# Expert stage of a one-core network: routing ahead of the token split, gathers of four experts, sixteen weight buffers, and a written order for TensorE

## The chip, the cores and the metric

The kernel runs as one program on one core of a Trainium2 chip. The metric is the device time of one execution in microseconds. The kernel before takes 2054.01 us, the median of 3 runs (2053.54 to 2054.9).

## The reference, cut to what matters

256 tokens of width 1024 go through a first block (two layers, each a gated feed-forward part, a mixer of a state space scan and dilated attention, and a second feed-forward part) and then a second block. The second block computes a hybrid mixer of a convolution and a gated linear attention, and ends like this:

```python
h = h + ga1[:, None, :] * y                 # y: the mixer's w_out product
u2 = modulate(rmsnorm(h, g_norm2[l]), sh2, sc2)
y2 = hierarchical_moe(u2, ...)              # 4 groups of 8 experts
h = h + ga2[:, None, :] * y2
...
return modulate(rmsnorm(h, g_final), shf, scf)

# in hierarchical_moe, t = u2 as 256 tokens:
gsel = top_k(t @ w_rg + b_rg, 1)            # a group for each token
top_v, top_i = lax.top_k(le_sel, TOP_K)     # two of the group's 8 experts
w = jax.nn.softmax(top_v, axis=-1) * wg
for e in range(N_EXPERTS):
    hid = jax.nn.silu(t @ w1[e]) * (t @ w3[e])
    y = y + comb[:, e:e + 1] * (hid @ w2[e])
```

There are 32 experts with a hidden width of 512, so w1, w3 and w2 of one expert are 2 MB each in fp32.

## The kernel before, in words

The dense part (first block, and the second up to `w_out`) streams fp32 weights through a ring of 1 MB buffers called `raw`, splits each in a high and a low part (`hi` on ScalarE, `lo` on VectorE) and sums three products in PSUM. The change leaves it nearly as it is. Its last product is `w_out` of the second block (in `mixer2`, from L957): two pieces of 512 columns, each of 256 token rows. Behind each piece come the residual (L968, L969), the product with the router's gain row (L971), the turn to columns on TensorE (L974) and the router's logits (L980). Then `rsqrt` gives the norm's factor on VectorE (three Newton steps, L84 to L86), and L989 scales the logits.

**Routing** (`route`, L1197) is one chain on VectorE over the 36 logits of each token: the best group, the best and second expert, their sum as a one-hot mask (L1234); two matmuls (L1237, L1238) count each token's place in its expert, and L1240 gives `pos`. **norm2** (L1329) writes the normed tokens `u` (L1335, the shift row `sh2` added), their high part `u2h` on ScalarE and the low part `u2l` on GpSimd (L1341). `moe_final` calls norm2 between the creation of the routing chain and its first step, and the instructions stand in that order on VectorE.

**The gather** (L1412): from `pos`, L1417 writes one-hot matrices `sel` for a batch of 8 experts with 64 slots each (512 columns). For each of 8 pieces of 128 features, four matmuls (`u2h` and `u2l`, two token halves, 512 columns) pick the tokens, and the result is copied to `T`. Four batches serve 32 experts.

**The experts** (L1530) are taken two at a time, 16 pairs. For each pair `project` runs w1 and w3 (L1469), `hidden` turns the results (L1484) and writes H with Silu and a product, and `down` runs w2 of the pair before (L1504). Its products have 64 slots as the stationary tile, the two experts side by side in the array. `spread` adds the results, as high and low part `yh` and `yl`, to the tokens with `selT` (L1522). A pair has 12 loads of 1 MB: two halves of two buffers (one for each expert) for each of w1, w3, w2. `halves` asks for two new loads when it has used two buffers:

```python
for i in range(2):
    yield i, (self.loaded.pop(0), self.loaded.pop(0))
    self.refill(2)
    self.tick()
```

The order on the engines is chosen by a scheduler at build time. Side work (gathers, `slots`, spreads) is handed to it as generators that `tick` advances beside the products.

**Weight buffers.** The 1 MB buffers of the expert stage are in four pools: RAW2 = 3 and RAW3 = 2 that open during the mixer, RAWB = 4 taken over from the dense ring, RAW4 = 3 that open when the dense part's memory is free: 12. A load is issued on SP's queue (L1392) when its buffer is free, in program order.

**The end.** `finish` (L1358) multiplies the sum by `ga2`, adds it to `x`, squares, `rsqrt`, and writes the output with the rows `Gf` and `shf`. `finish_rows` (L1343) loads these rows on GpSimd's queue right behind the routing and forms `Gf` there.

## Time and profile before

| | |
|---|---|
| median of 3 runs | 2054.01 us |
| profiled execution | 2053.34 us, its span 2051.6 us |
| PE busy | 1967.1 us (96%) |
| VectorE (DVE) busy | 1226.8 us (60%) |
| ScalarE (ACT) busy | 882.6 us (43%) |
| GpSimd (POOL) busy | 138.5 us (7%) |
| expert weights | 192 loads of 1024 KB |
| DMA in the last eight of 40 slices | 414 to 421 GB/s in six of them, 378 and 369 in the others but the last |

The expert stage begins at about 1524 us of the span. Ahead of it TensorE is the busy engine and the DMA moves 97 to 283 GB/s in a slice of 51 us; in it both are close to full. The page's share for PE is an average over both.

### The profile page before, as it was taken

How to read it: one execution, taken by the hardware profiler on the slowest of the kernel's cores; microseconds unless marked ns; L12 is line 12 of the kernel's file. 1: busy time of each engine (PE TensorE's matmuls, PEld its weight loads, DVE VectorE, ACT ScalarE, POOL GpSimd, SP SyncE). 2: the span in 40 equal slices, each digit the busy share in tenths (PEclk: the TensorE clock that was granted, in tenths of full speed). 3: DMA queues.
4: the chain of work that ended last, by engine and by line, in shares of the span. 5: the costliest groups of instructions: out<-in, count | busy, mean ns of one | idle time of the engine just before them, and what ended most of it. 6: DMA issues, size and time to landing. Idle time of an engine off the chain costs nothing. (4 is left out here: it accounts for less than half of the span.)

```text
span 2051.6 us, 25322 instructions
## 1 busy us (share of the span) xinstructions
PE 1967.1 (96%) x9734; PEld 1436.8 (70%) x9734; DVE 1226.8 (60%) x2099; ACT 882.6 (43%) x1318; POOL 138.5 (7%) x226
## 2 busy tenths in 40 slices
PE   8999999999999999999999999999969999999996
PEld 6888978788888888887788888978754333333332
DVE  5884897778867775698866555999772111110113
ACT  5444676654444444575745444576522101111101
POOL 1000222000000000014000000000120000000001
PEclk9999999999999999999999999999989999999998
DMA  8885543447776885642446556544766999999994
GB/s 281 280 283 185 166 144 103 154 155 266 263 258 207 266 271 182 196 150 97 133 144 204 179 164 204 177 148 140 244 261 269 422 414 378 421 369 420 421 421 172
DMA packets 193100, 493.11 MB, mean 240 GB/s; under 512 B 11832, under 2 KB 47600, under 8 KB 168400
## 3 DMA queue, kind: packets, MB, share of 16 engines
q1 hardware_dynamic: 185760, 479.32, 64.6%
q0 software_dynamic: 4992, 11.49, 1.7%
q8 instruction: 78, 1.28, 0.2%
q10 hardware_dynamic: 2224, 0.66, 0.2%
q14 instruction: 46, 0.38, 0.1%
HBM read 490.34 MB, written 1.08 MB: 240 GB/s over the span
## 5 line engine op out<-in xcount | busy, mean ns | idle before, releaser
L128 DVE TENSOR_TENSOR lo<-raw,hi 128x1024 fp32r<-128x1024 f32 (+1 forms) x462 | 563.6, 1221 | 280.4 <-ACT hi L127 279.4
L127 ACT ACTIVATE hi<-raw 128x1024 fp32r<-128x1024 f32 (+1 forms) x462 | 486.6, 1055 | 548.4 <-PE mm L174 477.9
L172 PE MATMUL mm<-hi,xh 128*128 128x512 f32 (+2 forms) x1200 | 463.9, 388 | 3.7 <-ACT hi L127 3.7
L173 PE MATMUL mm<-lo,xh 128*128 128x512 f32 (+2 forms) x1200 | 458.3, 382 | 0.4 <-DVE lo L128 0.4
L174 PE MATMUL mm<-hi,xl 128*128 128x512 f32 (+2 forms) x1200 | 457.8, 381 | 0.0
L172 PEld LDWEIGHTS mm<-hi,xh 128*128 128x128 f32 x1200 | 226.0, 189 | 49.2 <-ACT hi L127 4.6
L173 PEld LDWEIGHTS mm<-lo,xh 128*128 128x128 f32 x1200 | 226.2, 188 | 46.3 <-DVE lo L128 2.0
L174 PEld LDWEIGHTS mm<-hi,xl 128*128 128x128 f32 x1200 | 226.0, 188 | 46.0
L1469 PE MATMUL mm<-raw,T 128*64 128x512 f32 x1024 | 242.4, 596 | 0.0
L1469 PEld LDWEIGHTS mm<-raw,T 128*64 128x64 f32 x1024 | 72.9, 137 | 139.8 <-issue 137.0
L1504 PE MATMUL mm<-raw,H 128*64 128x512 f32 x512 | 148.6, 600 | 10.1 <-DVE gu L1474 10.1
L172 PE MATMUL mm<-hi,hh 128*128 128x512 f32 x352 | 139.1, 395 | 0.0
L174 PE MATMUL mm<-hi,hl 128*128 128x512 f32 x352 | 138.8, 394 | 0.0
L173 PE MATMUL mm<-lo,hh 128*128 128x512 f32 x352 | 138.5, 394 | 0.0
L1474 DVE COPY gu<-mm 128x512 f32<-128x512 f32 x16 | 11.1, 692 | 178.6 <-PE mm L1469 168.8
L1504 PEld LDWEIGHTS mm<-raw,H 128*64 128x64 f32 x512 | 45.9, 136 | 85.6 <-issue 63.3
L1512 ACT ACTIVATE yh<-mm,wsl 128x512 fp32r<-128x512 f32 x32 | 22.0, 687 | 181.7 <-PE mm L1504 181.7
L190 PE MATMUL mm<-xl,hi 128*128 128x256 f32 x320 | 90.0, 282 | 0.4 <-DVE xl L204 0.4
L189 PE MATMUL mm<-xh,hi 128*128 128x256 f32 x320 | 89.7, 282 | 0.0
L191 PE MATMUL mm<-xh,lo 128*128 128x256 f32 x320 | 89.7, 281 | 0.0
L759 DVE SCALAR_TENSOR_TENSOR macc<-raw,cact,macc 128x512 f32<-128x512 f32 x112 | 83.9, 750 | 2.2
L1513 DVE SCALAR_TENSOR_TENSOR yl<-mm,wsl,yh 128x512 fp32r<-128x512 f32 x32 | 24.0, 751 | 94.3 <-ACT yh L1512 93.0
(428 smaller groups left out, 2642.6 us busy)
## 6 DMA issues: line engine op xcount, KB each, us to landing
raw<-in_w_dram SPq DMA_DIRECT2D x192, 1024.0 KB, 10.2
raw<-in_w_in_dram SPq DMA_DIRECT2D x71, 1024.0 KB, 5.2
raw<-in_ffn_w_up_dram SPq DMA_DIRECT2D x44, 1024.0 KB, 7.0
raw<-in_ffn_w_gate_dram SPq DMA_DIRECT2D x43, 1024.0 KB, 5.2
raw<-in_ffn_w_down_dram SPq DMA_DIRECT2D x40, 1024.0 KB, 5.1
raw<-in_w_ada_dram SPq DMA_DIRECT2D x24, 1024.0 KB, 5.3
raw<-in_w_out_dram SPq DMA_DIRECT2D x20, 1024.0 KB, 5.1
raw<-in_w_ada_f_dram SPq DMA_DIRECT2D x8, 1024.0 KB, 5.3
```

The source lines that it names most:

```text
L127: nc.scalar.activation(h, r, AF.Copy)
L128: nc.vector.tensor_tensor(l, r, h.bitcast(F32), op=ALU.subtract)
L172: nc.tensor.matmul(ps[t][:, :w], xh[:, kc, sl], hi, start=kc == 0, stop=False)
L173: nc.tensor.matmul(ps[t][:, :w], xh[:, kc, sl], lo, start=False, stop=False)
L174: nc.tensor.matmul(ps[t][:, :w], xl[:, kc, sl], hi, start=False, stop=kc == kt - 1)
L189: nc.tensor.matmul(o, hi[:, sl], xh[:, kc, :], start=kc == 0, stop=False)
L190: nc.tensor.matmul(o, hi[:, sl], xl[:, kc, :], start=False, stop=False)
L191: nc.tensor.matmul(o, lo[:, sl], xh[:, kc, :], start=False, stop=kc == kt - 1)
L759: last = nc.vector.scalar_tensor_tensor(acc, raw[:, k, :], c, acc, op0=ALU.mult, op1=ALU.add)
L1469: nc.tensor.matmul(pg[s * CAP : (s + 1) * CAP, :], x[:, kc, s, :], w[:, k, :], start=kc == 0, stop=kc == KD - 1,)
L1504: nc.tensor.matmul(pd[nb][q, :], H[:, c, q], w[s][:, k, nb * 512 : (nb + 1) * 512], start=c == 0, stop=c == 3,)
L1513: nc.vector.scalar_tensor_tensor(yl, pd[nb], ws, yh.bitcast(F32), op0=ALU.mult, op1=ALU.subtract)
```

## The change

- Constants: a batch is 4 experts (256 columns for a gather), 16 weight buffers (RAW2 = 4, RAW4 = 6).
- `w_out` of the second block runs as 512, 256 and 256 columns, so the residual, turn and logits of the last piece have half the size. `rsqrt` has seven operations for its steps where it had nine.
- The routing chain stands right behind the logits. `u2h` is written from `xg` on ScalarE with the norm's factor as scale, in four pieces of 512, and `u2l` on VectorE (`low`) in four pieces of 512, one of them while TensorE counts places and three behind `sel`. The shift `sh2` is now a column of 128x8 and is added when a gather's PSUM result is copied to `T`. Nothing of this is on GpSimd.
- The first gather uses four PSUM banks at a time, `u2h` ahead of `u2l`.
- TensorE's order in the expert stage is the program's own (`manual_schedule`), and the side work stands at fixed hooks between halves. Spreads run behind the first half of the next pair's w1.
- `finish_rows` stands behind the last pair's projections, loads its rows on SP's queue into two buffers of the weight ring, and forms `Gf` with one VectorE operation per row. `finish` uses the memory of `u2h` and `u2l`.

```diff
-RAW2 = 3
+RAW2 = 4
 RAW3 = 2
-RAW4 = 3
-BATCH = 8
+RAW4 = 6
+BATCH = 4
...
-        for _ in range(3):
-            nc.vector.tensor_mul(t, y, y)
-            nc.vector.scalar_tensor_tensor(t, t, -0.5, m, op0=ALU.mult, op1=ALU.mult)
-            nc.vector.scalar_tensor_tensor(y, t, 1.5, y, op0=ALU.add, op1=ALU.mult)
+        nc.vector.tensor_mul(t, y, y)
+        nc.vector.scalar_tensor_tensor(t, t, -0.703952253 * RC, m, op0=ALU.mult, op1=ALU.mult)
+        nc.vector.scalar_tensor_tensor(y, t, 0.703952253 * 2.38924456 * RC, y, op0=ALU.add, op1=ALU.mult)
+        nc.vector.tensor_mul(t, y, y)
+        nc.vector.tensor_mul(t, t, m)
+        nc.vector.scalar_tensor_tensor(t, t, -10.0 / 3 * RC**2, t, op0=ALU.add, op1=ALU.mult)
+        nc.vector.scalar_tensor_tensor(y, t, 5.0 * RC**4, y, op0=ALU.add, op1=ALU.mult)
...
+            for i, (c0, w) in enumerate(((0, 512), (512, 256), (768, 256))):
+                sl = slice(c0, c0 + w)
+                n = w // P
+                ps = self.gemm_x(a["w_out_2"][0], c0, w, self.xh, self.xl)
...
-        nc.vector.tensor_add(mb, o1, o2)
+        done = nc.vector.tensor_add(mb, o1, o2).ins
 
         pp = self.t(self.mm, [P, 512], "mm")
         nc.tensor.matmul(pp[:, 0:64], self.tri_le, mb, start=True, stop=False)
         nc.tensor.matmul(pp[:, 32:64], self.ones, mb[:, 0, :], start=False, stop=True)
+        with self.tc.issue_after(done):
+            lows.pop(0)()
...
+        self.xg = self.t(self.s2, [P, 2, D], "T")
+        self.sh2 = self.t(self.const, [P, KD], "cact")
...
-            self.norm2(lp, u2h, u2l)
+            lows = self.norm2(u2h, u2l)
+            route = self.route(lp, lows)
             pos = next(route)
-            rows = self.finish_rows(lp)
-            comb, cnt = self.experts(lp, u2h, u2l, route, pos, acc)
+            with tc.manual_schedule(engines={mybir.EngineType.PE}):
+                comb, cnt, rows = self.experts(lp, u2h, u2l, lows, route, pos, acc)
...
-            nc.vector.scalar_tensor_tensor(
-                u.rearrange("p (k q) -> p q k", k=KD), self.xg[:, t, :].rearrange("p (q k) -> p q k", k=KD),
-                self.rstd[:, t : t + 1], self.sh2.rearrange("p (q k) -> p q k", k=KD),
-                op0=ALU.mult, op1=ALU.add,
...
+            return lambda: nc.vector.scalar_tensor_tensor(
+                l, u, r, h.bitcast(F32), op0=ALU.mult, op1=ALU.subtract
             )
-            nc.scalar.activation(u2h[:, t, :], u, AF.Copy)
-            nc.gpsimd.tensor_tensor(u2l[:, t, :], u, u2h[:, t, :].bitcast(F32), op=ALU.subtract)
-
-    def finish_rows(self, lp):
+
+        lows = []
+        for k0 in range(0, KD, 4):
+            for t in range(2):
+                h, l = (
+                    x[:, t, k0 * P : (k0 + 4) * P].rearrange("p (k q) -> p k q", k=4) for x in (u2h, u2l)
+                )
+                u = self.xg[:, t, :].rearrange("p (q k) -> p k q", k=KD)[:, k0 : k0 + 4, :]
+                r = self.rstd[:, t : t + 1]
+                nc.scalar.activation(h, u, AF.Copy, scale=r)
+                lows.append(low(h, u, l, r))
+        return lows
...
+            w = self.eraw().rearrange("p a b -> p (a b)").rearrange("p (k n) -> p k n", n=D)
+            rows += [w[:, 0, :], w[:, 1, :]]
...
+            nc.sync.dma_start(dst, self.modd[0:1, idx * D : (idx + 1) * D].to_broadcast([P, D]))
+        g = rows.pop()
+        nc.sync.dma_start(g, a["g_final_2"].rearrange("(o n) -> o n", o=1).to_broadcast([P, D]))
+        nc.vector.scalar_tensor_tensor(rows[1], rows[1], 1.0, g, op0=ALU.add, op1=ALU.mult)
...
-            self.tick()
-
-    def gather(self, pool, b, u2h, u2l, pos, out, banks=None):
+            for f in hooks[i] if hooks else ():
+                f()
...
+        with self.tc.issue_after(i.ins):
+            for low in lows:
+                low()
...
+        for k0 in range(0, KD, n_k):
+            pgs = banks or [self.t(self.tp, [P, 512], "tp")]
+            pgs = [x[:, : BATCH * CAP].rearrange("p (e s) -> p e s", e=BATCH) for x in pgs]
             for n, src in enumerate((u2h, u2l)):
-                for t in range(2):
-                    nc.tensor.matmul(
-                        pg, src[:, t, sl], sel[:, t], start=n == 0 and t == 0, stop=n == 1 and t == 1
-                    )
-            if kc % 2:
-                nc.vector.tensor_copy(T[:, kc], pg)
-            else:
-                nc.scalar.activation(T[:, kc], pg, AF.Copy)
+                for kc, pg in enumerate(pgs, k0):
+                    sl = slice(kc * P, (kc + 1) * P)
+                    for t in range(2):
+                        nc.tensor.matmul(
+                            pg, src[:, t, sl], sel[:, t], start=n == 0 and t == 0, stop=n == 1 and t == 1
+                        )
+            for kc, pg in enumerate(pgs, k0):
+                sh = self.sh2[:, kc : kc + 1]
+                if kc % 2:
+                    nc.vector.tensor_scalar(T[:, kc], pg, sh, None, op0=ALU.add)
+                else:
+                    self.filled = nc.scalar.activation(T[:, kc], pg, AF.Identity, bias=sh).ins
...
+            gu.append(self.project(pool, x, on_scalar, [spread], [some(gat, 2 if ei else 3)]))
+            if e == 0:
+                with self.tc.issue_after(filled):
+                    comb, combs, cnt = next(route)
+            slots = self.slots(pool, sel, ei, e, combs, so)
+            gu.append(
+                self.project(pool, x, nc.vector.tensor_copy, [some(turns, 1), some(slots, 1)], [])
+            )
             if last:
-                self.down(pool, e - 2, last[0][0], *last[1], acc)
-            for _ in hid:
-                pass
+                spread = self.down(
+                    pool, e - 2, last[0][0], *last[1], acc, [some(turns, 1), some(gat, 1)], [some(gat, 1)]
+                )
+            else:
+                next(turns)
             last = h, so
-        self.drain()
-        self.down(pool, NEXP - 2, last[0][0], *last[1], acc)
-        self.drain()
-        return comb, cnt
+        rows = self.finish_rows()
+        spread_end = self.down(pool, NEXP - 2, last[0][0], *last[1], acc, [spread], [])
+        spread_end()
```
TensorE, in a pair's w1/w3 and the w2 products of the pair before; `raw` is a weight buffer, `H` the hidden values, `mm` a PSUM result of one half of w2's columns, `tp` a turn or a gather. Before:

```order
L1504 MATMUL mm_14549<-raw_14434,H_14422 64x512
L1504 MATMUL mm_14550<-raw_14434,H_14422 64x512
L1484 MATMUL tp_14583<-csq_66,gu_14540 128x128 x4
L1446 MATMUL tp_14606<-identr_320,sel_13752 128x128 x2
L1448 MATMUL tp_14606<-combs_13699,sel_13752 128x4 x2
L1504 MATMUL mm_14549<-raw_14436,H_14422 64x512
L1504 MATMUL mm_14549<-raw_14434,H_14422 64x512
L1504 MATMUL mm_14549<-raw_14436,H_14422 64x512
L1504 MATMUL mm_14550<-raw_14436,H_14422 64x512
```
After:

```order
L1528 MATMUL mm_14061<-raw_13867,H_13876 64x512
L1528 MATMUL mm_14061<-raw_13869,H_13876 64x512
L1528 MATMUL mm_14061<-raw_13867,H_13876 64x512
L1528 MATMUL mm_14061<-raw_13869,H_13876 64x512
L1528 MATMUL mm_14062<-raw_13867,H_13876 64x512
L1528 MATMUL mm_14062<-raw_13869,H_13876 64x512
L1528 MATMUL mm_14062<-raw_13867,H_13876 64x512
L1528 MATMUL mm_14062<-raw_13869,H_13876 64x512
L1509 MATMUL tp_14075<-csq_66,gu_14059 128x128 x4
L1455 MATMUL tp_14081<-sel_13999,u2h_13613 128x256 x2
L1455 MATMUL tp_14081<-sel_13999,u2l_13614 128x256 x2
```
Before, the first two rows use the buffer of the same expert, and `raw_14434` and `raw_14436` (the two experts of the pair) alternate irregularly around the turns. After, the two buffers alternate in every row of a half, and turns and gathers stand between halves.

SP's queue where the last `w_out` weights and the first expert weights (`in_w_2`) are issued. Before:

```order
L156 DMA raw_13344<-in_w_out_dram 128x4x512
L156 DMA raw_13419<-in_w_out_dram 128x4x512
L1392 DMA raw_13152<-in_w_2_dram 128x2048
L1392 DMA raw_13154<-in_w_2_dram 128x2048
L1392 DMA raw_13156<-in_w_2_dram 128x2048
L156 DMA raw_13453<-in_w_out_dram 128x4x512
```
After:

```order
L162 DMA raw_13309<-in_w_out_dram 128x4x512
L1410 DMA raw_13115<-in_w_2_dram 128x2048
L1410 DMA raw_13117<-in_w_2_dram 128x2048
L1410 DMA raw_13119<-in_w_2_dram 128x2048
L1410 DMA raw_13121<-in_w_2_dram 128x2048
L162 DMA raw_13384<-in_w_out_dram 128x8x256
L162 DMA raw_13468<-in_w_out_dram 128x8x256
```
Four expert loads stand ahead of the last `w_out` loads where three stood, and these are two of 256 columns where one of 512 stood behind them.

VectorE from the logits `lg` to the one-hot `sel`. Before:

```order
L989 SCALAR_TENSOR_TENSOR lg_13536<-ax_13305,nw_y_13524,wr_13158 128x36
L989 SCALAR_TENSOR_TENSOR lg_13536<-ax_13306,nw_y_13524,wr_13158 128x36
L1335 SCALAR_TENSOR_TENSOR T_13580<-T_13150,nw_y_13524 128x128x8 x2
L1211 TENSOR_REDUCE rgm_13588<-lg_13536 128x2
L1212 TENSOR_TENSOR gu_13587<-lg_13536,rgm_13588 128x8
```
After:

```order
L998 SCALAR_TENSOR_TENSOR lg_13565<-ax_13271,nw_y_13555,wr_13123 128x36
L1220 TENSOR_REDUCE rgm_13620<-lg_13565 128x2
...
L1243 TENSOR_TENSOR gu_13619<-gu_13619 128x64
L1346 SCALAR_TENSOR_TENSOR u2l_13614<-T_13112,nw_y_13555,u2h_13613 128x512
L1251 TENSOR_TENSOR pos_13648<-mm_13644,gu_13619 128x64
L1436 TENSOR_TENSOR sel_13652<-cmisc_316,pos_13648 128x256 x2
L1346 SCALAR_TENSOR_TENSOR u2l_13614<-T_13112,nw_y_13555,u2h_13613 128x512 x3
```
The two L1335 operations ahead of the chain are gone; one `u2l` piece stands in front of `pos`, in the time of the count on TensorE, and three stand behind the first `sel`.

## Rows read from the trace of the kernel before

**Rows 1.** The page: its first line, and the DMA issues (x, KB, us to landing).
```profile
span 2051.6 us, 25322 instructions
...
raw<-in_w_dram SPq DMA_DIRECT2D x192, 1024.0 KB, 10.2
```
**Rows 2.** Busy time by stretch: length, PE, PEld, DVE, ACT, POOL, PEclk, DMA share, GB/s.
```profile
1528.00:1556.00 28.00, 15.60 (x62) 10.45 (x64) 18.06 (x41) 5.91 (x11) 11.05 (x8) 0.68 0.07 19
1556.00:1560.00 4.00, 4.00 (x22) 1.40 (x20) 0.32 (x2) 0.60 (x1) 0.00 (x0) 1.00 0.99 340
1800.00:1900.00 100.00, 94.85 (x395) 36.06 (x392) 12.36 (x22) 10.05 (x17) 0.00 (x0) 1.00 0.97 394
1900.00:2010.00 110.00, 104.94 (x453) 39.78 (x454) 12.10 (x23) 11.81 (x20) 0.00 (x0) 1.00 1.01 421
2018.60:2020.00 1.40, 1.40 (x9) 0.56 (x6) 0.00 (x0) 0.00 (x0) 0.00 (x0) 1.00 0.26 105
```
**Rows 3.** PE's timeline at the start of the expert stage: start us, us, what.
```profile
1539.75 0.69 PE L1237 MATMUL mm<-gu,csq 128*128 128x64 f32 x2 [15.69 <-DVE gu L1234]
...
1551.36 3.65 PE L1469 MATMUL mm<-raw,T 128*64 128x512 f32 x16
```
**Rows 4.** DVE's timeline from the last residual to the one-hot matrices.
```profile
1516.30 0.69 DVE L968 TENSOR_TENSOR xg<-mm,gain 128x512 f32<-128x512 f32 x1 [7.45 <-PE mm L174]
...
1523.09 0.16 DVE L86 SCALAR_TENSOR_TENSOR nw_y<-nw_t,nw_y 128x2 f32<-128x2 f32 x1
...
1524.27 3.77 DVE L1335 SCALAR_TENSOR_TENSOR T<-T,nw_y 128x1024 f32<-128x1024 f32 x2
...
1528.10 2.05 DVE L1212 TENSOR_TENSOR gu<-lg,rgm 128x8 f32<-128x8 f32 x1
...
1533.99 0.22 DVE L1212 TENSOR_TENSOR gu<-gu,r1m 128x64 f32<-128x64 f32 x1
...
1539.47 0.22 DVE L1234 TENSOR_TENSOR gu<-gu 128x64 f32<-128x64 f32 x1
...
1541.11 1.29 DVE L1417 TENSOR_TENSOR sel<-cmisc,pos 128x512 fp32r<-128x512 f32 x2
```
**Rows 5.** POOL's timeline beside it.
```profile
1527.40 5.02 POOL L1341 TENSOR_TENSOR u2l<-T,u2h 128x1024 fp32r<-128x1024 f32 x2 [6.09 <-ACT u2h L1340]
```
**Rows 6.** PE's timeline in the steady expert stage.
```profile
1715.41 1.07 PE L1504 MATMUL mm<-raw,H 128*64 128x512 f32 x2 [0.78 <-DVE gu L1474]
...
1717.43 7.08 PE L1504 MATMUL mm<-raw,H 128*64 128x512 f32 x28
...
1727.70 7.09 PE L1469 MATMUL mm<-raw,T 128*64 128x512 f32 x32
1735.47 0.74 PE L1484 MATMUL tp<-csq,gu 128*128 128x128 f32 x4 [0.68 <-ACT gu L1534]
...
1744.01 1.07 PE L1504 MATMUL mm<-raw,H 128*64 128x512 f32 x2 [0.78 <-DVE gu L1474]
...
1861.40 0.75 PE L1484 MATMUL tp<-csq,gu 128*128 128x128 f32 x4 [0.68 <-ACT gu L1534]
```
**Rows 7.** PE's timeline where matmuls have 256 columns, in the dense part.
```profile
207.67 0.28 PE L189 MATMUL mm<-xh,hi 128*128 128x256 f32 x1
207.79 0.28 PE L190 MATMUL mm<-xl,hi 128*128 128x256 f32 x1
```
**Rows 8.** All engines' timeline at the end.
```profile
2024.91 7.09 PE L1504 MATMUL mm<-raw,H 128*64 128x512 f32 x30
...
2033.43 2.56 DVE L1365 TENSOR_TENSOR T<-acc,fin 128x512 f32<-128x512 f32 x4
...
2045.51 2.74 DVE L1377 SCALAR_TENSOR_TENSOR T<-T,nw_y,fin 128x512 f32<-128x512 f32 x4 [0.21 <-DVE nw_y L86]
```
**Rows 9.** Busy time by stretch, columns as in rows 2.
```profile
1860.00:1870.00 10.00, 8.54 (x41) 2.83 (x38) 0.69 (x1) 1.19 (x2) 0.00 (x0) 1.00 1.01 418
1521.90:1545.80 23.90, 7.32 (x23) 6.24 (x24) 19.55 (x40) 4.70 (x8) 11.65 (x8) 0.50 0.31 122
```

More of the change, by code (lines that the diff above doesn't have):

```diff
@@ L27 @@
 NEXP = 32
+RC = 0.375**0.2
 CAP = 64
@@ L983, in mixer2 @@
                         )
-                if nb == 0:
+                if i == 0:
                     self.moe_more()
-            self.prep_end()
+            s2 = self.t(self.small, [P, 2], "ss2", bufs=2)
+            nc.vector.tensor_reduce(s2, ss, axis=AX.X, op=ALU.add)
+            self.rstd = self.rsqrt(s2, 2, 1.0 / D)
             self.lg = self.t(self.small, [P, 2, 36], "lg", bufs=1)
@@ L1345, in finish_rows @@
+        return lows
+    def finish_rows(self):
         nc, a = self.nc, self.a
-        rows = [self.t(lp, [P, D], f"fin{j}") for j in range(3)]
+        rows = []
+        for _ in range(2):
+            w = self.eraw().rearrange("p a b -> p (a b)").rearrange("p (k n) -> p k n", n=D)
+            rows += [w[:, 0, :], w[:, 1, :]]
         for dst, idx in zip(rows, (5, 7, 6)):
-            nc.gpsimd.dma_start(dst, self.modd[0:1, idx * D : (idx + 1) * D].to_broadcast([P, D]))
-        g = a["g_final_2"].rearrange("(o n) -> o n", o=1)
@@ L1350, in finish_rows @@
-        for nb in range(2):
-            sl = slice(nb * 512, (nb + 1) * 512)
-            gr = self.t(lp, [P, 512], "gu", bufs=4)
-            nc.gpsimd.dma_start(gr, g[:, sl].to_broadcast([P, 512]))
-            nc.gpsimd.tensor_scalar(rows[1][:, sl], rows[1][:, sl], 1.0, None, op0=ALU.add)
-            nc.gpsimd.tensor_mul(rows[1][:, sl], rows[1][:, sl], gr)
+            nc.sync.dma_start(dst, self.modd[0:1, idx * D : (idx + 1) * D].to_broadcast([P, D]))
+        g = rows.pop()
+        nc.sync.dma_start(g, a["g_final_2"].rearrange("(o n) -> o n", o=1).to_broadcast([P, D]))
@@ L1360, in finish @@
         ga2, Gf, shf = rows
-        yz = self.t(pool, [P, 4, D], "T")
-        y, z = yz[:, 0:2, :], yz[:, 2:4, :]
+        y = self.t(pool, [P, 2, D], "u2h")
+        z = self.t(pool, [P, 2, D], "u2l")
         parts = [(t, nb, slice(nb * 512, (nb + 1) * 512)) for t in range(2) for nb in range(2)]
@@ L1403, in expert_loads, with halves @@
         yield from of("w2_2", NEXP - 2, 4)
-    def halves(self):
+    def halves(self, hooks=()):
         for i in range(2):
@@ L1409, in halves, with gather @@
             self.refill(2)
-            self.tick()
-    def gather(self, pool, b, u2h, u2l, pos, out, banks=None):
+            for f in hooks[i] if hooks else ():
+                f()
+    def gather(self, pool, b, u2h, u2l, pos, out, banks=None, lows=()):
         nc = self.nc
@@ L1459, in slots, with project @@
         yield
-    def project(self, pool, x, copy):
+    def project(self, pool, x, copy, *hooks):
         nc = self.nc
         pg = self.t(self.mm, [P, 512], "mm")
-        for i, raws in self.halves():
+        for i, raws in self.halves(hooks):
             for k in range(4):
@@ L1518, in spread, with experts @@
         def spread():
-            for nb in range(2):
-                for t in range(2):
-                    for n, y in enumerate(ys[nb]):
-                        nc.tensor.matmul(
-                            acc[t][nb], selT[:, t * P : (t + 1) * P], y,
-                            start=e == 0 and n == 0, stop=e == NEXP - 2 and n == 1,
-                        )
-                yield
-        return self.beside(spread())
-    def experts(self, pool, u2h, u2l, route, pos, acc):
+            for t, nb in ((0, 0), (0, 1), (1, 0), (1, 1)):
+                for n, y in enumerate(ys[nb]):
+                    nc.tensor.matmul(
+                        acc[t][nb], selT[:, t * P : (t + 1) * P], y,
+                        start=e == 0 and n == 0, stop=e == NEXP - 2 and n == 1,
+                    )
+        return spread
+    def experts(self, pool, u2h, u2l, lows, route, pos, acc):
         nc = self.nc
@@ L1534, in on_scalar, with some, none @@
             nc.scalar.activation(d, s, AF.Copy)
-        batch, last = [], None
-        nxt = self.beside(self.gather(pool, 0, u2h, u2l, pos, batch, acc[0] + acc[1]))
-        sel0 = next(nxt[0])
+        def some(gen, n):
+            return lambda: [next(gen, None) for _ in range(n)]
+        def none():
+            pass
+        batch, last, spread = [], None, none
+        gat = self.gather(pool, 0, u2h, u2l, pos, batch, acc[0] + acc[1], lows)
         for e in range(0, NEXP, 2):
```

105 lines of the change are left out of this document (44 added, 61 removed).

## The prediction, made before the changed kernel ran

> **What bounds the kernel now.** I read the page first, then busy times by stretch, then the timelines of PE and VectorE through the expert stage, and the end last. The page puts PE at 96% of the span, but that is mostly the dense part, which the change leaves as it is but for its tail. The expert stage is another case: it must move 192 loads of 1.0486 MB [rows 1], and between 1900 and 2010 us the DMA moves 421 GB/s with PE busy 104.94 of 110 us [rows 2]. One load costs 1.0486/421 = 2.491 us there, a pair of experts (12 loads) 29.9 us. PE needs almost the same for a pair: 1744.01 − 1715.41 = 28.6 us without a gather [rows 6], and from 1735.47 to 1861.40, four pairs with one gather in them, 125.93/4 = 31.5 us [rows 6]. So neither hides the other: where a gather makes PE late, buffers come free late and the DMA falls to 394 GB/s [rows 2].
>
> Ahead of this the DMA stands still: from 1528 to 1556 us it moves 19 GB/s [rows 2], because all 12 buffers are full and the first product that frees any starts at 1551.36 [rows 3]. The chain to that product is on VectorE: last residual at 1516.30, norm's factor done at 1523.09 + 0.16 = 1523.25, L1335 until 1528.04, routing chain until the mask at 1539.47 + 0.22 = 1539.69, `sel` from 1541.11 [rows 4]. PE idles 15.69 us for the mask [rows 3].
>
> At the end the last load has landed at about 1 us behind 2018.6, as the share of 0.26 in the next 1.4 us shows [rows 2]; I take 2018.6. PE's last w2 product ends at 2024.91 + 7.09 = 2032.0 [rows 8], 13.4 us later; the span ends 2051.6 − 2032.0 = 19.6 us behind that.
>
> **The change part by part, on the time line of the profiled execution.**
>
> *PE's pair.* A run of 32 records that alternates the two experts takes 7.09 us, 0.2216 each; the w2 run of 28 takes 7.08 where 28 would take 6.20 [rows 6], so written alternation takes 0.88 off. The two lone runs of 2 take 1.07 each for 0.44 [rows 6]: 1.26 off. The waits of 0.68 (for ScalarE's Silu result and copies, L1534) and 0.78 (for VectorE's copy, L1474) in front of them [rows 6]: 1.46 off, since after the change a half of w2 or w1 stands between a projection's end and its turn, 16 records or 3.5 us, more than either wait. Together 28.6 − 0.88 − 1.26 − 1.46 = 25.0 us. Half a gather falls to each pair: 16 matmuls of 256 columns, which follow each other every 207.79 − 207.67 = 0.12 us [rows 7], 1.9 us; and about three more breaks between kinds of work at some 0.2 us (half of 1.07 − 2 × 0.2216 = 0.63 [rows 6] is 0.3, as the upper end): 0.6. PE's pair becomes 25.0 + 1.9 + 0.6 = 27.5 us, under the DMA's 29.9. Bounds: 26 (no breaks, gather hidden in them) to 31.1 (nothing saved, 28.6 + 2.5). The DMA sets the pace up to 29.9 in any case.
>
> [...]
>
> *The start.* The last `w_out` piece has half the columns: three operations of about 0.69 for each of two token halves [rows 4] become 0.4, 1.8 us off (bounds 1 to 2.1, half of 6 × 0.69); two fewer `rsqrt` steps of 0.2: 0.4 off. So the factor is at 1523.25 − 2.2 = 1521.05 and the logits are scaled at 1521.7 (0.65 later, an estimate; L1335 began 1.02 us behind the factor). L1335 no longer stands in front of the chain: its 3.77 us go. The chain itself took 1539.69 − 1528.04 = 11.7 us. Its first 128x8 operation took 2.05 us while GpSimd wrote `u2l` for 5.02 us [rows 4, 5]; one on 128x64, eight times the size, took 0.22 in the same chain [rows 4]. Its work on the final rows followed. I read this as VectorE slowed by GpSimd, which has nothing to do there after the change: 18 operations at 0.26 and two small ones moved in give 5.0 us. Bounds: 4 (18 at 0.22) to 11.7 (no relief). Mask at 1526.7; `sel` follows 1.4 us later as before (1541.11 − 1539.69), the `u2l` piece being hidden in the count: 1528.1, 1529 if it is not.
>
> From `sel` to the first product it was 1551.36 − 1541.11 = 10.25 us [rows 3, 4]. The gather now has half the columns, its `sel` half the size, but three `u2l` pieces of 0.65 (half of a 128x1024 of 1.29, the size of the `sel` pair [rows 4]) to 0.94 (a quarter of L1335's 3.77) stand on VectorE behind `sel`, and the `u2l` products wait for them. Half of 10.25 is 5.1; the unchanged time 10.25; I take the middle, 7.5. First product at 1535.6, 15.8 us earlier. `u2h` on ScalarE costs nothing: it starts at the factor, with routing (5.7 us) to cover it, and is late by at most two of four pieces, inside that bound.
>
> *DMA.* Before, the stream came back 1556.0 − 1551.36 = 4.64 us behind the first product, after a half of w1 [rows 2, 3]; now at 1540.2. With 16 buffers filled, 176 loads remain instead of 180. RAW4 buffers open when the dense part ends at about 1517: six loads, 15 us, full by 1533, so that the gap is some 7 us. The four loads ahead of the last `w_out` weights on SP's queue cost nothing as long as those land before their product: the fourth adds 2.5 us of transfer, if shared evenly, to weights that the last 7 us of `w_out` products need; 0 to 2.5, I take 0. The remaining stream is 176 × 2.491 = 438.4 us plus 0.8 for its start (4 us at 340 in place of 421 GB/s [rows 2]): last load at 1979.4. Before, 180 loads took 2018.6 − 1556.0 = 462.6 where 448.4 would do; 14.2 us were lost to late buffers.
>
> *From the last load to the end.* PE, ahead of the DMA, does the last half, 16 records at 0.2216 = 3.6 us and 0.3 to start: 1983.3. PE's own bound is 16 pairs without the first gather (2 × 1.9): 1535.6 + 440 − 3.8 = 1971.8, 11.5 us of slack. Then 19.6 us as before, 0.4 less for `rsqrt` and about 2.35 more: `Gf` is one VectorE operation per row, 1.4 us (two halves of 0.69 [rows 4]), `finish_rows` loads 2 MB behind the last weights, 5 us of stream, of which `ga2` (the first) is there when L1365 would start and `Gf`'s must be by then, 8 us behind the last load; the last `yl` in front of it and the second buffer's wait are the other 0.95. Bounds for this term: −0.4 to 6 (rows 5 us late and one operation). So the span is 1983.3 + 19.6 − 0.4 + 2.35 = 2004.85 us.
>
> As differences: 10.0 for four loads more ahead, 15.8 for the earlier start, 13.4 for the stream without losses (14.2 less 0.8), 9.5 for PE's lag at the end (13.4 − 3.9), −1.95 for the tail; 46.75 from 2051.6. The profiled execution was 2053.34, 1.74 around its span, and 0.67 under the median of the runs: 2004.85 + 1.74 + 0.67 = 2007.3, **2007 us**.
>
> **Rivals.** *The order buys nothing for PE.* The breaks stay, for instance because w1 and w2 products with different stationary operands cost them, and a pair is 31.1 us. For it: the runs that alternate were already 7.09 us. Against: the runs that don't are 14% dearer a record. PE would be the bound: 1971.8 + 16 × 3.6 = 2029.4, + 21.55 (to the end) + 2.41 (to the runs' median) = 2053 us, no measurable change.
>
> *PE waits in its written order: slower.* Before, the scheduler could put other work in front of a late copy; now PE stops. A pair has about six handovers between PE and the engines that empty PSUM; if each waits 0.73 us (the mean of 0.68 and 0.78 [rows 6]), a pair is 27.5 + 4.4 = 31.9 us, the end at 1971.8 + 16 × 4.4 + 21.55 + 2.41 = 2066 us. It decides from 31.4 us a pair on, where the time is over 2058. Against it: two PSUM banks of each kind, and 3.5 us of other products between result and use.
>
> *Routing isn't slowed by GpSimd.* The chain stays near 11.7 us, `sel` and gather no shorter; the first product is at 1549, the last load at 1992.8, the time 2021 us.
>
> *The clock falls.* With PE waiting for 2.4 us of each 29.9, the granted clock may fall to 0.50, the lower level, as from 1521.90 to 1545.80, where PE was busy 7.32 of 23.9 us; from 1860 to 1870, with 8.54 of 10 us busy, it stayed at 1.00 [rows 9]. At half clock a pair takes up to 55 us: 1535.6 + 2 × 436.2 + 24 = 2432 us. The waits here are short and PE stays near 92% busy, so I give it little. [...]
>
> **How the numbers follow.** My forecast has 0.74, routing unrelieved 0.12, order without gain 0.07, waits in order 0.05, clock 0.02. The forecast's own range is 1996 to 2018: the start may be 3 us earlier or 5 later, a stream between 417 and 425 GB/s is 4 us either way, the tail −2.7 to +3.7. The range of 8 in 10 takes in unrelieved routing and part of the way to the PE-bound case: 1996 to 2028. A measurement of this kernel tells 0.2%, some 4 us, from no change. Faster: 0.74 + 0.12 + about half of the third = 0.90; same: the other half and the edge of the fourth, 0.04; slower: 0.06.
>
> **What would show it.** In the profile after: a stretch of low DMA rate of about 7 us in place of 28, near 1533 to 1540; first expert product at 1535.6; routing operations on 128x8 at 0.2 to 0.3 us; then 421 GB/s without a dip until about 1979; PE waiting for weights some 2.4 us a pair, with w2's 32 records near 7.1 us; 21.5 us from the last product to the end. I am wrong if PE never waits for a load in the steady stage, if the first product is later than 1545, or if DMA stays under 410 GB/s while buffers are free.

## The result and the profile after

The changed kernel takes 2009.69 us, the median of 4 runs (2007.2 to 2011.22), against 2054.45 of the kernel before (now of 4 runs): a ratio of 0.978, 95% interval 0.9763 to 0.9797, faster by 2.2%. The forecast was 2007 us. The profiled execution took 2007.2 us, its span is 2005.3.

Busy time by stretch of the changed kernel (columns as in rows 2):

```profile
1533.00:1537.50 4.50, 4.50 (x23) 1.54 (x23) 2.15 (x10) 2.38 (x6) 0.00 (x0) 1.00 0.04 18
...
1600.00:1700.00 100.00, 100.00 (x484) 42.14 (x485) 16.61 (x33) 14.32 (x26) 0.00 (x0) 1.00 1.01 421
...
1800.00:1900.00 100.00, 99.14 (x454) 45.68 (x451) 13.36 (x27) 12.47 (x23) 0.00 (x0) 1.00 1.01 421
1900.00:1975.00 75.00, 72.07 (x300) 29.61 (x301) 9.95 (x19) 8.41 (x15) 0.00 (x0) 1.00 1.02 421
```

The stretch of 28 us at 19 GB/s [rows 2] is now 4.5 us at 18, and the stream moves 421 GB/s in every stretch of the steady stage, where 394 stood in one before [rows 2]. The granted clock is 1.00 from the first product to the last (1533 to 1984), beside the waits for weights too.

Its timeline at the start, VectorE and the first product (start us, us, what):

```profile
1515.38 0.43 DVE L975 TENSOR_TENSOR xg<-mm,gain 128x256 f32<-128x256 f32 x1 [5.02 <-PE mm L180]
...
1521.05 0.17 DVE L1221 TENSOR_TENSOR gu<-lg,rgm 128x8 f32<-128x8 f32 x1
...
1524.93 0.22 DVE L1243 TENSOR_TENSOR gu<-gu 128x64 f32<-128x64 f32 x1
1525.08 1.15 DVE L1346 SCALAR_TENSOR_TENSOR u2l<-T,nw_y,u2h 128x512 fp32r<-128x512 f32 x1
...
1526.57 0.76 DVE L1436 TENSOR_TENSOR sel<-cmisc,pos 128x256 fp32r<-128x256 f32 x2
...
1533.18 7.09 PE L1495 MATMUL mm<-raw,T 128*64 128x512 f32 x32
```

These lines answer to [rows 3, 4]: the mask is there at 1525.15 (1539.69 before), `sel` starts at 1526.57 (1541.11), the first product at 1533.18 (1551.36). The 128x8 operation that took 2.05 us takes 0.17. Where the first gather began, from 1526 to 1529, the granted clock was 0.50; ahead of it PE had waited 5.47 us for the mask. Eight of its products took 2.17 us there, and eight took 1.07 us from 1532.18 on, when the granted clock was 1.00.

PE in one steady pair, from a turn to the same turn of the next pair:

```profile
1619.12 0.75 PE L1509 MATMUL tp<-csq,gu 128*128 128x128 f32 x4
...
1623.62 3.60 PE L1528 MATMUL mm<-raw,H 128*64 128x512 f32 x16
...
1628.31 3.65 PE L1528 MATMUL mm<-raw,H 128*64 128x512 f32 x16
...
1646.49 0.75 PE L1509 MATMUL tp<-csq,gu 128*128 128x128 f32 x4
```

A pair is 1646.49 − 1619.12 = 27.4 us with its half gather (31.5 as a mean before [rows 6]), in which w2's 32 records (a product leaves two: the page has 512 of L1528 for 256 products) are two runs of 3.60 and 3.65 without a wait in front of the turns.

The end:

```profile
1974.82 3.65 PE L1528 MATMUL mm<-raw,H 128*64 128x512 f32 x14 [0.39 <-DMA raw<-in_w_dram]
...
1978.40 0.50 PE L1545 MATMUL acc<-yh,selT 128*128 128x512 f32 x1
...
1980.45 3.65 PE L1528 MATMUL mm<-raw,H 128*64 128x512 f32 x16
...
1987.95 1.22 DVE L1373 SCALAR_TENSOR_TENSOR raw<-raw,raw 128x1024 f32<-128x1024 f32 x1
...
1998.94 2.74 DVE L1395 SCALAR_TENSOR_TENSOR u2l<-u2h,nw_y,raw 128x512 f32<-128x512 f32 x4 [0.21 <-DVE nw_y L92]
```

The last w2 half ends at 1980.45 + 3.65 = 1984.1 (2032.0 before [rows 8]), and the span ends 21.2 us later (19.6 before).

### The profile page after: what moved, and what is told of

It is laid out like the page before. It is cut to its first block, busy times and chain, and to the rows that moved or that the text cites. A ratio compares the mean times of both kernels' runs of the same rounds, so it can differ in the third digit from the quotient of the medians.

```text
span 2005.3 us, 25668 instructions
## 1 busy us (share of the span) xinstructions
PE 1947.7 (97%) x9910; PEld 1449.0 (72%) x9910; DVE 1221.3 (61%) x2090; ACT 890.5 (44%) x1342; POOL 125.0 (6%) x215
## 5 line engine op out<-in xcount | busy, mean ns | idle before, releaser
L178 PE MATMUL mm<-hi,xh 128*128 128x512 f32 (+1 forms) x1216 | 467.0, 386 | 3.2 <-ACT hi L133 3.2
L179 PE MATMUL mm<-lo,xh 128*128 128x512 f32 (+1 forms) x1216 | 461.4, 379 | 0.2 <-DVE lo L134 0.2
L180 PE MATMUL mm<-hi,xl 128*128 128x512 f32 (+1 forms) x1216 | 460.5, 379 | 0.0
L1528 PE MATMUL mm<-raw,H 128*64 128x512 f32 x512 | 125.2, 597 | 3.4 <-DMA raw<-in_w_dram 3.4
L1461 DVE TENSOR_SCALAR T<-tp,cact 128x256 f32<-128x256 f32 x28 | 13.5, 483 | 137.1 <-PE tp L1455 137.1
L1528 PEld LDWEIGHTS mm<-raw,H 128*64 128x64 f32 x512 | 42.4, 137 | 71.4 <-issue 51.2
L180 PEld LDWEIGHTS mm<-hi,hl 128*128 128x128 f32 x352 | 66.2, 188 | 15.3
L179 PEld LDWEIGHTS mm<-lo,hh 128*128 128x128 f32 x352 | 66.2, 188 | 15.0
```

Of the source, the lines that this page charges most:

```text
L178: nc.tensor.matmul(ps[t][:, :w], xh[:, kc, sl], hi, start=kc == 0, stop=False)
L179: nc.tensor.matmul(ps[t][:, :w], xh[:, kc, sl], lo, start=False, stop=False)
L180: nc.tensor.matmul(ps[t][:, :w], xl[:, kc, sl], hi, start=False, stop=kc == kt - 1)
L1461: nc.vector.tensor_scalar(T[:, kc], pg, sh, None, op0=ALU.add)
L1528: nc.tensor.matmul(pd[nb][q, :], H[:, c, q], w[s][:, k, nb * 512 : (nb + 1) * 512], start=c == 0, stop=c == 3,)
```

## The experiments

Times are medians (of two runs for the four-and-four kernel and the two with a break, of four or more for the others); the changed kernel is 2009.7. Runs of one code differ by up to 4 us, and the last residual (L975) stands anywhere from 1515.0 to 1518.0 in profiles where nothing ahead of it was edited; differences of 2 us are not read.

**Twelve buffers.**

```diff
-RAW2 = 4
+RAW2 = 3
-RAW4 = 6
+RAW4 = 3
```

> The changed kernel with 12 weight buffers as before (RAW2 3, RAW4 3) and all else kept. My theory: in the expert stage the weight stream sets the pace, so each buffer that is full before the first product takes one load of 2.49 us off the stream behind it; four fewer cost 4 x 2.49 = 10.0 us (2019.7 where the changed kernel takes 2009.7), the first product stays at 1533 us and the pair stays at 29.9 us of stream. Rival: PE's pace sets the end and the buffers only let the stream run ahead of it; then PE, 11.5 us or more ahead at the end, covers it and the time moves by less than 3 us. Second rival: 12 buffers are too few for PE's burst and the stream dips below 415 GB/s in the steady stage; then over 15 us.

Measured: 2018.96 us (ratio 0.9832, 0.9815 to 0.9848), 9.3 us over the changed kernel; spans 2015.6 and 2005.3. Its stretch while the buffers are full:

```profile
1526.00:1537.00 11.00, 10.21 (x50) 7.51 (x52) 7.80 (x20) 3.73 (x8) 0.00 (x0) 0.72 0.01 1
```

The stream stands for these 11 us where it stood for 4.5, with the first product at the same place (1533.30). A buffer that is full before the first product is worth nearly a load (2.3 us of 2.49), as the first theory has it; behind it the stream keeps 421 GB/s, so neither rival holds.

**The order left to the scheduler.**

```diff
-            with tc.manual_schedule(engines={mybir.EngineType.PE}):
+            with ExitStack():
```

> The changed kernel with TensorE's order left to the scheduler in the expert stage (no written order; hooks, buffers, routing kept). Its order has 56 places where two products of the same expert follow each other, where the written order has none and the kernel before 57. My theory: each such place costs PE the overlap of the two array halves, about 0.43 us, and there are 14 more breaks of 0.3: 28 us of PE's time, of which about 16 are slack against the stream, so some 12 us slower (5 to 20), with PE's pair near 29 us. Rival: the written order matters little since the stream sets the pace; no change within 3 us. Second rival: the written order is the main source of the gain and PE's pair goes back to 31 us: 40 us slower.

Measured: 2068.53 us (1.0068, 1.0052 to 1.0085): 59 us over the changed kernel, and slower than the kernel before. All three expectations missed; the second rival is nearest. PE around w2 in one pair:

```profile
1661.78 1.07 PE L1528 MATMUL mm<-raw,H 128*64 128x512 f32 x2 [0.78 <-DVE gu L1500]
1662.79 0.75 PE L1509 MATMUL tp<-csq,gu 128*128 128x128 f32 x4
...
1664.63 3.65 PE L1528 MATMUL mm<-raw,H 128*64 128x512 f32 x12
...
1669.96 1.93 PE L1528 MATMUL mm<-raw,H 128*64 128x512 f32 x4
...
1672.13 3.65 PE L1528 MATMUL mm<-raw,H 128*64 128x512 f32 x12
...
1695.77 1.07 PE L1528 MATMUL mm<-raw,H 128*64 128x512 f32 x2 [0.78 <-DVE gu L1500]
```

The pair takes 1695.77 − 1661.78 = 34.0 us. Twelve records take the 3.65 us that sixteen take in the changed kernel, four take 1.93. Waits of PE for VectorE and ScalarE (0.78 us here, 0.31 and 0.68 elsewhere in the pair) are 1.8 of the 6.6 us that the pair is longer than in the changed kernel. Most of the rest hangs on how runs are cut, and the next runs ask by what.

**Neighbours of one expert in w2.**

```diff
-                for k in range(2):
-                    c = 2 * i + k
-                    for s in range(2):
+                for s in range(2):
+                    for k in range(2):
+                        c = 2 * i + k
```

> The changed kernel with w2's products written so that two of the same expert follow each other (128 such places, 8 a pair), nothing else changed. My theory: 8 x 0.43 = 3.4 us more for a pair, 30.9 us on PE against 29.9 of stream, so that PE becomes the bound: 16 x 3.4 = 55 us less the slack of 16, about 39 us slower (25 to 50). Rival: the price of a place is only what the lone groups before showed beyond their fill, 0.2 us; then a pair is 29 us, the stream stays the bound and the time moves by at most 5 us.

Measured: 2008.12 us (0.9779, 0.9763 to 0.9796), no change. A half of w2 with its products as A A B B A A B B:

```profile
1624.42 3.65 PE L1528 MATMUL mm<-raw,H 128*64 128x512 f32 x16
```

(A and B are the two experts of the pair.) My theory fell: two in a row of the same expert cost nothing, 3.65 us for 16 records as in the changed kernel. The rival gave the time, but not by the price it named. The run lengths of the second experiment suggested another, an estimate of mine: 1.07, 1.93, 3.65 and 7.09 us fit 0.853 times the larger count of the two experts (1, 2, 4, 8 products), and some 0.24. By that a break costs where the counts on its two sides are uneven. Three kernels were made for this.

**Four and four.** w1, w3 and w2 written as A A A A B B B B in every half:

```diff
-            for k in range(4):
-                kc = 4 * i + k
-                for s, w in enumerate(raws):
+            for s, w in enumerate(raws):
+                for k in range(4):
+                    kc = 4 * i + k
...
-            for nb in range(2):
-                for k in range(2):
-                    c = 2 * i + k
-                    for s in range(2):
+            for s in range(2):
+                for nb in range(2):
+                    for k in range(2):
+                        c = 2 * i + k
```

> The changed kernel with every half of w1, w3 and w2 written as four products of one expert and then four of the other. My theory after the first runs (balance): between two breaks, PE works the two halves of its array side by side whatever the order, and a run takes 0.853 us times the larger of the two experts' counts and 0.24; the halves are 4 and 4, 3.65 us as now, and the time does not move (within 5 us of 2009.7). Rival (order): a product waits for the one ahead of it on the same half of the array and holds up the ones behind; then only the last of the first four and the first of the second overlap, a half takes 7 x 0.853 + 0.24 = 6.2 us, a pair 15.4 us more, and the time is about 230 us longer.

Measured: 2155.9 us (1.0495, 1.0474 to 1.0516), 146 us over, between the two.

```profile
1533.92 8.97 PE L1495 MATMUL mm<-raw,T 128*64 128x512 f32 x32
...
1661.85 5.42 PE L1528 MATMUL mm<-raw,H 128*64 128x512 f32 x16
```

5.42 us less 0.24 is 6.1 times 0.853: not 4 (balance alone) and not 7 (strict order). Two lengths stand beside it: A A B B A A B B took 3.65 us, as measured above, and A A A A B B B B twice over without a break, the first run of this kernel with 32 records, took 8.97. Why four in a row cost what they do is not shown.

**An uneven break, and an even one.** The turn of the w3 result is moved into w2's first half. In the first kernel the halves of w2 are written A A A A B B B B and the turn stands after A A A A; in the second they are A A B B A A B B and it stands after A A B B. The lines that place the turn:

```diff
+                if i == 0 and s == 0:
+                    mid()
...
+                if i == 0 and nb == 0:
+                    mid()
```

> The changed kernel with each half of w2 written as four products of one expert and four of the other, and the turn of the w3 result put between them in the first half (it stood behind that half). Balance theory: the break leaves 4 and 0 on either side, two runs of 4 x 0.853 + 0.24 = 3.65 us where one was, 15 pairs x 3.65 = 55 us on PE, less its slack of 16: about 39 us slower (30 to 50), PE's pair 31 us. Rival: a break costs only its own start of 0.24 us wherever it stands; no change within 4 us.

> The changed kernel with the same turn put in the middle of w2's first half, but that half written by columns, so that two products of each expert stand on either side. Balance theory: two runs of 2 x 0.853 + 0.24 = 1.95 us for one of 3.65, 0.24 us a pair, hidden by the slack: no change within 4 us. Rival: any break inside a half costs what the split costs; then as slow as that, about 39 us.

Measured: 2087.69 us (1.0163, 1.0143 to 1.0183) for the uneven break, 78 us over; 2008.15 (0.9776, 0.9756 to 0.9795) for the even one, no change. The uneven one:

```profile
1645.58 5.42 PE L1528 MATMUL mm<-raw,H 128*64 128x512 f32 x16
...
1652.94 3.65 PE L1495 MATMUL mm<-raw,T 128*64 128x512 f32 x16 [1.28 <-issue]
...
1671.37 3.60 PE L1528 MATMUL mm<-raw,H 128*64 128x512 f32 x8
1674.90 0.75 PE L1509 MATMUL tp<-csq,gu 128*128 128x128 f32 x4
1675.58 3.65 PE L1528 MATMUL mm<-raw,H 128*64 128x512 f32 x8
```

The even one:

```profile
1654.08 1.94 PE L1528 MATMUL mm<-raw,H 128*64 128x512 f32 x8
1655.94 0.75 PE L1509 MATMUL tp<-csq,gu 128*128 128x128 f32 x4
1656.62 1.94 PE L1528 MATMUL mm<-raw,H 128*64 128x512 f32 x8
```

Eight records on either side of the same break take 3.6 us each where they are of one expert and 1.94 where they are two and two. The uneven kernel is dearer than expected: its second half, A A A A B B B B without a break, takes 5.42 (what the four-and-four kernel showed), 1.8 us more a pair, and in front of the next w1 PE stands idle for 1.28 us, for which the profile names no engine. The expectation had left out both.

**GpSimd beside VectorE.** Six subtractions of 128x512 into an unused tile; in a first version they started too early and lay beside `w_out`:

```diff
+            junk = self.t(lp, [P, D // 2], "junk")
+            for _ in range(6):
+                nc.gpsimd.tensor_tensor(junk, self.xg[:, 0, : D // 2], self.xg[:, 1, : D // 2], op=ALU.subtract)
```

> The changed kernel with six extra GpSimd subtractions of 128x512 into an unused tile, that start when the last residual is done and lie beside routing. My theory (routing before was slow because GpSimd worked beside VectorE): routing operations on 128x8 and 128x64 that now take 0.17 to 0.23 us take 1 to 2 us at several places again, the chain from the logits to the mask goes from 4.3 to 8 to 11 us, the first product comes 4 to 7 us later and the time is 4 to 7 us longer. Rival: the chain's length was its own (its order or the L1335 in front of it); then routing stays at 4.3 us and the time does not move.

Measured: 2013.51 us (0.9797, 0.978 to 0.9813). Routing was as fast as without (4.3 us; GpSimd was done by then), but the last residual came at 1521.98, 6.6 us later than in the changed kernel's profile, and the span was 6.7 us longer. By the medians the time is 3.8 us longer, just short of the 4 to 7 expected, and at another place. The second version reads the columns `D // 2 :`, which the last residual writes:

> The changed kernel with the same six GpSimd subtractions of 128x512, now reading the columns that the last residual writes, so that they start at about 1518 us and lie beside routing (in the run before they had run beside the w_out splits and made VectorE's operations of 128x256 take up to 1.4 us in place of 0.42, the last residual 6.6 us late). My theory (GpSimd slows VectorE): single operations of routing take 1 to 2 us, the chain from logits to mask 7 to 11 us in place of 4.3, the span 3 to 7 us longer. Rival: routing's small operations are not touched; the chain stays at 4.3 us and the time does not move.

Measured: 2014.36 us (0.9804, 0.9787 to 0.982), 4.7 us over the changed kernel; spans 2012.9 and 2005.3. Its timeline:

```profile
1520.70 7.99 POOL L1336 TENSOR_TENSOR junk<-T 128x512 f32<-128x512 f32 x6 [45.89 <-ACT sq L984]
1520.90 1.09 DVE L79 TENSOR_SCALAR nw_m<-ss 128x2 f32<-128x2 f32 x1
1522.02 0.17 DVE L82 TENSOR_SCALAR nw_t<-nw_m 128x2 int32<-128x2 int32 x1
1522.22 1.11 DVE L83 TENSOR_SCALAR nw_y<-nw_t 128x2 int32<-128x2 int32 x1
1523.37 0.16 DVE L86 TENSOR_TENSOR nw_t<-nw_y 128x2 f32<-128x2 f32 x1
```

GpSimd's work fell on `rsqrt` and ended as the chain from the logits began (4.55 us in place of 4.30: its first 128x8 operation, the last beside GpSimd, took 0.40 in place of 0.17). In `rsqrt`, operations on 128x2 take 1.1 and 0.16 us in turn: five of them lose some 0.94 us each, 4.7 us. That the medians differ by the same 4.7 us is partly chance: in this profile the last residual stands at 1517.93, 2.55 us later than in the changed kernel's, where nothing was edited. With it the first product is 7.5 us later (1540.67) and the span 7.6 us longer. So GpSimd's work does slow VectorE's small operations, and in these profiles a later start is a later end, one for one.

**The kernel before without GpSimd beside routing.** The call of `finish_rows` also moves behind `experts`:

```diff
-            nc.gpsimd.tensor_tensor(u2l[:, t, :], u, u2h[:, t, :].bitcast(F32), op=ALU.subtract)
+            nc.vector.tensor_tensor(u2l[:, t, :], u, u2h[:, t, :].bitcast(F32), op=ALU.subtract)
...
-            nc.gpsimd.tensor_scalar(rows[1][:, sl], rows[1][:, sl], 1.0, None, op0=ALU.add)
-            nc.gpsimd.tensor_mul(rows[1][:, sl], rows[1][:, sl], gr)
+            nc.vector.tensor_scalar(rows[1][:, sl], rows[1][:, sl], 1.0, None, op0=ALU.add)
+            nc.vector.tensor_mul(rows[1][:, sl], rows[1][:, sl], gr)
```

> The kernel before with GpSimd's work beside routing given to VectorE: the two u2l subtractions and the operations on the final rows (the latter's program place moved behind the experts). Nothing else of the change is in it. My theory: routing's own operations take 0.16 to 0.23 us each, the chain from L1335's end to the mask goes from 11.7 us to about 8 (4.6 for routing, 2.4 for u2l and 0.9 for a row that stand in it), the first product comes 3 to 4 us earlier, and since PE with its 31.5 us a pair is what the end waits for in this kernel, all of it shows: 2050 us, 0.2% faster. Rival: the weight stream sets this kernel's end; 12 full buffers less a shorter gap give the same, so also 3 to 4 us, but with the dips of the stream unchanged in number. Second rival: the chain does not get shorter; no change.

Measured: 2051.32 us, ratio 0.9981 (0.9971 to 0.999). VectorE in routing, and the first product:

```profile
1530.45 0.16 DVE L1212 TENSOR_TENSOR gu<-lg,rgm 128x8 f32<-128x8 f32 x1
1532.73 0.43 DVE L1354 TENSOR_SCALAR fin<-fin 128x512 f32<-128x512 f32 x1 [2.13 <-DMA fin<-modd]
...
1548.48 3.65 PE L1469 MATMUL mm<-raw,T 128*64 128x512 f32 x16
```

The 128x8 operation takes 0.16 us where it took 2.05 beside GpSimd [rows 4], and no operation of the chain on 128x8 or 128x64 takes over 0.23. That is the plainest sign that GpSimd had slowed routing. The first product is 2.9 us earlier [rows 3], and the span is 2.8 shorter. The gain is there although VectorE does more, and although it waits 2.13 us in the chain for the load of a row. It does not tell the theory from the first rival, which forecast the same.

**Gathers of eight, with twelve buffers.**

```diff
-BATCH = 4
+BATCH = 8
```

> The changed kernel with 12 buffers (as the first experiment, 2019.0) and gathers of eight experts (512 columns) in place of four. My theory: in the steady stage the same columns are gathered, the stream keeps its 29.9 us a pair and hides them; only the first gather counts, twice as many columns: 32 matmuls of 512 and copies of 0.69 in place of 0.48 us, so the first product comes 3 to 5 us later than at 1533.3 and the time is 3 to 5 us longer than that of the first experiment, 2022 to 2024. Rival: the longer gathers, done within two of four pairs, make PE late (25.5 + 7.4 = 33 us a pair against 29.9) and with 12 buffers the stream dips below 410 GB/s; then over 10 us longer.

Measured: 2023.58 us (0.9849, 0.9833 to 0.9865), 4.6 us over the first experiment (2018.96).

```profile
1537.55 7.09 PE L1495 MATMUL mm<-raw,T 128*64 128x512 f32 x32
```

The first product is 4.25 us later than there, and the stream keeps 421 GB/s from 1550 on: gathers of four gain at the first gather only.

**Two versions made from this.** The second edits the end alone, the first has also a 17th buffer and starts w1 after half of the first gather. Core of the edits:

```diff
-RAW3 = 2
+RAW3 = 3
...
+            start = [spread] if e else [some(first, 1), lambda: fills.append(self.filled)]
+            gu.append(self.project(pool, x, on_scalar, start, [some(gat, 2 if ei else 3)]))
...
+        for nb in range(2):
+            for s in range(2):
+                raw = self.eraw()
+                src = a["w2_2"][0, NEXP - 2 + s].rearrange("(p k) n -> p k n", k=4)
+                self.nc.sync.dma_start(raw, src[:, :, nb * 512 : (nb + 1) * 512])
```

> A version made from the findings: the changed kernel with a 17th weight buffer (RAW3 3, room from one gu buffer less), the first half of w1 started after half of the first gather (that half copied by ScalarE alone), and the end as in the run beside it. My theory: the stream's gap of 4.2 us at 1533.3 to 1537.5 nearly closes (17th buffer 2.5, earlier first half 2), so the last load lands about 4 us earlier, and the end gives 4 to 6: 8 to 10 us faster than the changed kernel, 2000 to 2002 us. Rival: the stream stands still anyway behind the first loads, because the second gather half and its copies delay the next buffers; then only the end's part shows.

> The changed kernel with only the end changed: w2 of the last pair loaded and multiplied by column halves, so that the first half's results are spread and multiplied with ga2 while the last weights come; the rows for Gf loaded second; GpSimd's product with Gf given to VectorE. My theory: of the 21.2 us behind the last w2 product some 4 to 6 go (one yh and yl 1.4, half a spread 1, two products with ga2 1.4, GpSimd's locks 1.3): 2004 to 2006 us. Rival: 2 KB pieces of rows make the last four loads slower, and the rows that come behind them are what VectorE waits for; then no gain.

Measured: 2005.76 us (0.976, 0.9747 to 0.9774) and 2006.65 (0.9768, 0.9754 to 0.9781): 3.9 and 3.0 us under the changed kernel's median, with intervals that overlap its own. Less than forecast in both. No run shows the "locks" for which the sum of the second has 1.3 us; what the traces show is that the four additions to `x` took 4.65 us in the changed kernel, three of them beside GpSimd's products with `Gf`, and 2.50 in the first version, where VectorE does the products behind them. In the second, the last loads are in pieces of 2 KB. Its stream at the end, and PE:

```profile
1974.00:1978.00 4.00, 3.14 (x13) 0.96 (x14) 0.75 (x1) 0.69 (x1) 0.00 (x0) 1.00 1.05 388
...
1975.98 3.65 PE L1616 MATMUL mm<-raw,H 128*64 128x512 f32 x14 [0.86 <-DMA raw<-in_w_dram]
...
1981.77 0.51 PE L1627 MATMUL acc<-yh,selT 128*128 128x512 f32 x1
...
1983.45 3.65 PE L1616 MATMUL mm<-raw,H 128*64 128x512 f32 x16
```

The last w2 run ends at 1987.1 and the span 17.4 us later, where it was 21.2: the end itself is 3.8 us shorter, as intended. But the last run ends 3.0 us later than in the changed kernel (1984.1), so the span is only 0.8 us shorter (2004.5 against 2005.3). The run before it starts 1.2 us later, behind a wait for its load; the stream runs at 388 GB/s there, where the changed kernel had 417. That the pieces are the reason is argued only, as the rows are loaded in another order, and the first product was 0.7 us later. The other 1.8 us are PE's own order: four products that add the first columns (L1627, from 1981.77 on) now stand in front of the last run, which then waits for no load. In the first, the stream's gap only moved behind the first half of w1, as its rival said:

```profile
1533.00:1536.00 3.00, 3.00 (x14) 1.23 (x14) 0.88 (x3) 1.17 (x3) 0.00 (x0) 0.81 0.72 300
1536.00:1539.00 3.00, 3.00 (x21) 1.86 (x18) 0.00 (x0) 0.08 (x1) 0.00 (x0) 1.00 0.25 44
```

Its profile is one with the last residual at 1518.02, so what the edits at the start gave can't be told from that shift.

## Why the prediction was right, step by step

- *What bounds the kernel.* Right: the stream at 421 GB/s sets the pace after the change. It holds 421 GB/s from 1541 to 1975, and four buffers taken away cost 9.3 us where 10.0 was the sum's term.
- *PE's pair.* 27.4 us against 27.5. The reason was put wrongly. The step said that "written alternation takes 0.88 off"; neighbours of the same expert cost nothing when there are two (3.65 us a run, 2008.12 in all), and what the written order saves is breaks at places where the two experts' counts are uneven (two runs of 3.6 us there, of 1.94 at an even place). The size came out because it was read from runs whose lengths already held that. Without the written order, the new code takes 34.0 us a pair, more than the 31.1 that the rival of an order without gain had; that the smaller gathers make more breaks to be put at uneven places is a guess.
- *The start.* First product at 1533.18 against 1535.6. The last residual was 0.9 us earlier than before, which was not in the sum; routing took 4.3 us (5.0 forecast), `sel` to first product 6.6 (7.5 forecast). A `u2l` piece took 1.15 us, above the upper bound of 0.94 that I had from L1335; why is not shown. (`yl`, L1537, an operation of the same kind and size that reads PSUM, takes 0.75; `u2l` reads every eighth element of `xg`.) The other terms made up for it, by luck.
- *GpSimd as the reason of slow routing.* Borne out by the second GpSimd run, on other operations (1.1 us in place of 0.16), and directly by the kernel before without it: its 128x8 operation takes 0.16 us, and it gains 2.9 us at the start although the two `u2l` operations were moved into VectorE's chain.
- *The stream.* The gap was 4.5 us, not 7: the first product came 2.4 us earlier. The last load landed between 1974.82 and 1980.45, where 1979.4 was forecast; when exactly is not to be seen, since the 2 MB of rows share the stream from 1962 on.
- *PE's waits.* The check "PE waiting for weights some 2.4 us a pair" was wrong for most of the stage: PE's first idle time before a load is 0.42 us ahead of 1845.53. PE starts with 16 full buffers, 40 us of stream, and gains 29.9 − 27.4 = 2.5 us on it in a pair; it needs most of the stage to catch up. After that a pair takes what the stream takes (1845.53 to 1875.34 is 29.8 us), 2.4 more than PE needs, as foreseen; the profile marks 0.4 to 1.3 us of this a pair as idle time, and the rest lies in runs that take longer.
- *The end.* 1984.1 and 21.2 us, against 1983.3 and 21.55. That the first is so close is partly luck: the stream came back at about 1537.5, 2.7 us earlier than forecast, and the last product still ended 0.8 us later. The run of w2 before the last waited for its load until 1974.82, and the spread (eight products, from 1978.40 on) stood between it and the last run, which the sum had left out. The `Gf` operation took 1.22 us between the products with `ga2`.
- *The rivals.* Waits in the written order: one of 0.91 us in the first pair, none in the steady stage. Routing that GpSimd does not slow: its sum was wrong by its own terms, 1521.7 + 11.7 + 1.4 + 10.25 = 1545.1 for the first product and not 1549, so 2017 us and not 2021. The clock: 1.00 granted from the first product on, though a pair lost 2.4 us of 29.8 to waits from 1845 on; PE's idle times there are 0.4 to 0.9 us each. What longer ones would do in the expert stage was not shown.

Of the 2.7 us between forecast and median, 0.45 is the span (2005.3 against 2004.85); the rest lies in the runs, of which the profiled one was the fastest.

## What to carry to other kernels

Where a stream of weights sets the pace, count what stands in front of it. Here each full buffer was worth 2.3 us of a load's 2.49, and a first product 7.5 us later made the span 7.6 us longer, with PE at 27.4 us a pair against the stream's 29.9. When two small products stand side by side on PE, write the order so that every break falls where both have had the same number: an even break left two runs of 1.94 us, an uneven one two of 3.6. Alternation as such is not needed: two in a row cost nothing here (3.65 us), four did (5.42). Keep elementwise work on GpSimd away from a chain of small VectorE operations, which took 1.1 us in place of 0.16 beside it.

## What the runs showed of the hardware

- Four products of one expert alone took 3.60 us (the uneven break). Four of each of two experts, with 64 slots each side by side, took 3.65 together, alternating (the changed kernel) as well as two by two (A A B B A A B B). Two of each took 1.94 (the even break). Written as A A A A B B B B, four of each took 5.42.
- In the second GpSimd run, beside six GpSimd subtractions of 7.99 us together, five VectorE operations on 128x2 took 1.09 to 1.11 us each, and the five that stand in turn with them 0.16 or 0.17; in the changed kernel, without GpSimd there, all ten took 0.16 or 0.17. In the kernel before, an operation on 128x8 took 2.05 us beside two GpSimd operations of 5.02 together, and 0.16 in the same kernel without them.
